# A two-layer decoder trunk on one core: where the stream's known part, the last keys and values, and the background products are queued

## The chip, the cores and the metric

One core of a Trainium2 chip runs the whole program. The metric is the device time of one execution in microseconds (us); the time given for a kernel is the median of several runs. The engines are called as in the profile: PE does matmuls (PEld is its loading of weights), DVE and ACT work elementwise, POOL does a few small things, and SP issues most of the loads from main memory.

## The reference

Batch 1, 256 tokens, width 2048, two layers, all in 32-bit floats. Layer 0 mixes by causal pooling, layer 1 by latent attention with 16 heads; both have a gated feed-forward part of inner width 5632. Each layer gets six modulation vectors from a conditioning vector `c`.

```python
sc = silu(c)
for i in range(2):
    shift_m, scale_m, gate_m, shift_f, scale_f, gate_f = split(sc @ mod_w[i] + mod_b[i], 6)
    if i == 1:
        kv_shift, kv_scale = split(sc @ kv_mod_w + kv_mod_b, 2)
        h_kv = modulate(rmsnorm(x, kv_in_norm), kv_shift, kv_scale)
        ckv = rmsnorm(h_kv @ w_dkv, kv_norm)
        k_nope, v, k_rope = ckv @ w_uk, ckv @ w_uv, rope(h_kv @ w_kr)
    h = modulate(rmsnorm(x, norm_mix[i]), shift_m, scale_m)
    if i == 0:
        y = pool_mixer(h, pool_w, pool_scale)
    else:
        cq = rmsnorm(h @ w_dq, q_norm)              # the query's latent
        q_nope, q_rope = split(cq @ w_uq); q_rope = rope(q_rope)
        p = softmax(causal((q_nope @ k_nope.T + q_rope @ k_rope.T) * SM_SCALE))
        y = (p @ v) @ w_o
    x = x + gate_m * y
    h = modulate(rmsnorm(x, norm_ffn[i]), shift_f, scale_f)
    x = x + gate_f * ((silu(h @ ffn_gate[i]) * (h @ ffn_up[i])) @ ffn_down[i])
return rmsnorm(x, final_norm)
```

## The kernel before

**Products in three parts.** A weight block of 512 x 512 is loaded by SP into one of six `raw` buffers and split: ACT writes an upper half (L440, a rounding to a matmul format), DVE the rest (L442, the difference). The activations are split likewise. A product is then the sum of upper x upper, upper x lower and lower x upper. One such block for both tiles of 128 tokens is 24 matmuls of 128 x 512 (`proj_unit`, L464): 16 need the upper half of the weight, and the last 8 the lower one. There are six buffers for halves, which is three blocks.

**The order of the work.** Outside of a few stretches that are ordered by hand, a scheduler in the compiler orders each engine's instructions ahead of time: it plays the program with modelled durations and lets each engine take, of those ready, the instruction that comes first in the program; some are marked as more urgent (the splits by 100 places). What it has ordered is a fixed queue on the chip. `tc.issue_after(ins)` says that what a block traces on the engine of `ins` is queued behind `ins`; it is an order in the queue and not a wait for the end of `ins`.

**Background.** The modulation vectors are computed on DVE beside the products: a unit loads 128 rows of a modulation weight and adds them, times one element of silu(c), to an accumulator (L230; L305 twice for a smaller block). A vector of 2048 has 16 units. When the last is done, `folded` sums the accumulator over partitions: four pieces on DVE (L320, L321) and then one small matmul (L326). The units stand in a list. Each split calls `tick`, which adds a rate to a credit and starts a unit for each whole credit; `plan(left, units)` sets the rate so that the list gets down to `left` within `units` splits, `hold` stops it, `release` goes on with a new rate. `behind` holds at most one instruction behind which units are queued. What must come later but is not urgent goes to `pending`; each split's `flush` runs what has come due, queued behind its two halves, and counts the rest down by one.

**The feed-forward part** runs over 11 chunks of 512 (`project_chunk`: gate, then up, four blocks each), turns them, and multiplies groups of them with the down weights (`down`), once per group and per 512 columns of the output. The sums of the groups go to `x`, whose old content is kept in memory beside (`aside`). At the start of the last chunk, `StreamEnd` loads the old stream back into `parts`. In the last group, `known` makes of each piece of 512 columns and 128 tokens what is known before the last products: `x * gate` (L673), added to the old stream (L674). `piece` then adds the last products. In the code, `known` stands at the last down-projection: for the first columns at its start, for the next ones behind the first split of each column block.

**Between the layers** (`then_attention`, ordered by hand) comes the key and value latent. Its norm and halves are made by the class `Latent`: the sum of squares on ACT (L1312), a power on POOL (L1314), a scaling on DVE (L1315), a turn on PE (L606), upper halves on ACT (L1325), lower halves on DVE (L1327). Then `keys_values(g)` makes the keys (`head_T`, L1363, 48 matmuls of 128 x 256) and values (24 of L464) of four heads at a time, g = 0 to 3. `hidden_q` turns and modulates one of four pieces of the hidden state for the queries; `modulated` first runs everything that is pending. The order in the code is: keys and values 0 and 1; keys 2; `last_of_background`, with the first `hidden_q`; values 2; the second `hidden_q`; the rotary key; the four blocks of `w_dq` (the query's latent) with the other two pieces; the latent's norm; keys 3; the latent's turn and halves (`query_latent`); values 3.

**The heads** go in eight pairs. For a pair, `project_heads` makes queries, with their rotary part through `rope_start` (ACT copies from PSUM, L912 and L914) and `rope_end` (DVE, L918, L919, L921); `probabilities` makes scores and softmax of each head (L1459 to L1477: exponentials on ACT, L1472 and L1473; a reciprocal on DVE, L1475; scaling on both); `turned` and `output` follow one pair later. The loop runs, for pair g: scores and softmax of g, turning of g-1, queries of g+2, output of g-1. The background is held while the first two pairs' queries are made, and then released.

After the heads come the output projection, whose sums are multiplied with the gate row `mla` (L736), and layer 1's feed-forward part.

## Time and profile before

| | us |
|---|---:|
| median of 3 runs (lowest, highest) | 1936.26 (1934.76, 1936.73) |
| the profiled execution's own time | 1935.94 |
| its span, first to last instruction | 1934.20 |
| PE busy | 1866.6 |
| DVE busy | 1482.1 |
| ACT busy | 849.2 |
| POOL busy | 49.4 |

The mean granted clock of PE is 0.983 over the span. Times in the profile count from the start of the span. In a line of groups stand the kernel's line, engine, operation, what is written and read, the shapes and the count; behind the bar the busy time in us and the mean duration of one in ns; then the engine's idle time just ahead of these instructions and what ended it. In a line of the timeline or of the chain stand the start, the time taken, and what ran. In a line of waits: who waited for whom, us in total, how often, the longest. A line by stretch has the stretch, its length and the busy time of each engine with the number of instructions; asked for one line of the kernel alone, it has only that line's. A pair of instructions in a row on DVE starts a little less apart than the duration of one.

### The profile page before, as it was taken

Reading aid. Unit: us, or ns where it says so; the run is one execution under the profiler, and the core shown is the slowest. Engines: PE = TensorE matmul, PEld = TensorE weight load, DVE = VectorE, ACT = ScalarE, POOL = GpSimd, SP = SyncE. Lnnn points to the kernel's source line nnn. Section 1 sums busy time; section 2 is a strip of 40 time slices with the busy share of each in tenths; the row PEclk is TensorE's granted clock in tenths of the full one; section 3 lists DMA queues with packets and bytes.
Section 4 is the critical chain, followed back from the end, with each engine's and each line's share of the span. In section 5 each row is a group of like instructions: output and inputs, shape, how many; then the busy total and the mean of one; then the engine's idle time right before and its main releaser. Section 6 shows DMA issues by size and latency. Waiting matters only on the chain.

```text
span 1934.2 us, 22338 instructions
## 1 busy us (share of the span) xinstructions
PE 1866.6 (97%) x8836; PEld 1511.7 (78%) x8836; DVE 1482.1 (77%) x1419; ACT 849.2 (44%) x954; POOL 49.4 (3%) x46
## 2 busy tenths in 40 slices
PE   6689999999999999999999999999999999999998
PEld 3156887888888888787879888888888888888887
DVE  2148899999878788888799986989886565555656
ACT  3024634443433344335678735634444433333333
POOL 0000000000000000001200000000000000000000
PEclk9689999999999999999999999999999999999999
DMA  9999999889898999998698695998886667666651
GB/s 397 411 416 387 386 364 320 303 308 362 322 344 318 339 336 331 353 337 273 214 341 297 213 332 187 386 334 312 279 291 239 231 240 255 235 205 236 218 196 44
DMA packets 226114, 575.08 MB, mean 297 GB/s; under 512 B 12109, under 2 KB 16709, under 8 KB 203859
## 3 DMA queue, kind: packets, MB, share of 16 engines
q1 hardware_dynamic: 225482, 570.49, 81.5%
q0 software_dynamic: 432, 3.15, 0.4%
q8 instruction: 69, 1.13, 0.2%
q14 instruction: 35, 0.29, 0.0%
q10 hardware_dynamic: 96, 0.02, 0.0%
HBM read 567.31 MB, written 6.32 MB: 297 GB/s over the span
## 4 chain that ended last, share of the span: by engine, by line
PE 89%; DMA 5%; DVE 3%; ACT 2%; issue 1%; POOL 0%; SPq 0%; POOLq 0%; DVEq 0%; ACTq 0%
PE ps L464 77%; DMA raw<-in_mod_w_dram 4%; PE ps L473 2%; PE ps L1048 2%; PE ps L1363 2%; PE ps L274 1%; PE ps L798 1%; DVE hl L442 1%; DMA act<-in_x_dram 1%; DVE acc L230 1%; PE ps L1271 1%; DMA raw<-in_ffn_up_dram 0%; PE ps L606 0%; PE ps L1023 0%; PE ps L840 0%
## 5 line engine op out<-in xcount | busy, mean ns | idle before, releaser
L464 PE MATMUL ps<-hl,act 128*128 128x512 f32 x6744 | 1549.7, 391 | 6.9 <-DVE hl L442 4.3
L464 PEld LDWEIGHTS ps<-hl,act 128*128 128x128 f32 x6744 | 1266.2, 188 | 271.5 <-DVE hl L442 5.2
L440 ACT ACTIVATE hl<-raw 128x2048 fp32r<-128x2048 f32 x289 | 552.9, 1917 | 619.9 <-PE ps L464 505.4
L442 DVE TENSOR_TENSOR hl<-raw,hl 128x2048 fp32r<-128x2048 f32 x289 | 660.7, 2288 | 201.4 <-ACT hl L440 200.6
L230 DVE SCALAR_TENSOR_TENSOR acc<-raw,s_col,acc 128x2048 f32<-128x2048 f32 x112 | 262.8, 2346 | 0.7 <-DMA raw<-in_mod_w_dram 0.6
L305 DVE SCALAR_TENSOR_TENSOR acc<-raw,s_col,acc 128x1024 f32<-128x1024 f32 x112 | 143.4, 1280 | 2.2 <-DMA raw<-in_mod_w_dram 0.7
L274 PE MATMUL ps<-raw,front 128*32 128x512 f32 x392 | 66.6, 744 | 25.6 <-DMA raw<-in_mod_w_dram 25.5
L767 DVE TENSOR_TENSOR act<-ps,act 128x512 f32<-128x512 f32 x96 | 64.1, 684 | 10.5 <-PE ps L464 10.2
L274 PEld LDWEIGHTS ps<-raw,front 128*32 128x32 f32 x392 | 9.7, 119 | 60.9 <-DMA raw<-in_mod_w_dram 48.4
L1363 PE MATMUL ps<-act,hl 128*128 128x256 f32 x384 | 48.8, 284 | 0.0
L473 PE MATMUL ps<-hl,act 128*128 128x512 f32 x192 | 47.0, 399 | 1.2 <-DVE act L569 0.9
L1363 PEld LDWEIGHTS ps<-act,hl 128*128 128x128 f32 x384 | 47.5, 192 | 0.7 <-DVE act L1327 0.2
L801 ACT ACTIVATE act<-ps 128x512 fp32r<-128x512 f32 x44 | 23.8, 595 | 52.6 <-PE ps L798 45.0
L281 DVE COPY t2k<-ps 128x256 f32<-128x256 f32 x4 | 1.7, 424 | 57.5 <-ACT t2k L280 57.5
L856 DVE TENSOR_TENSOR x<-ps,x 128x512 f32<-128x512 f32 x32 | 22.1, 691 | 30.1 <-PE ps L464 30.1
L473 PEld LDWEIGHTS ps<-hl,act 128*128 128x128 f32 x192 | 35.1, 188 | 10.9 <-ACT act L556 1.8
L867 ACT ACTIVATE t2k<-ps 128x512 f32<-128x512 f32 x24 | 14.2, 592 | 62.6 <-PE ps L464 62.5
L493 ACT ACTIVATE junk<-x 128x512 bf16<-128x512 f32 x23 | 14.6, 633 | 60.7 <-DVE x L681 39.9
L871 DVE TENSOR_TENSOR t2k<-ps,t2k 128x512 f32<-128x512 f32 x24 | 16.5, 688 | 25.3 <-PE ps L464 25.3
L1048 PEld LDWEIGHTS ps<-act,act 128*128 128x128 f32 x128 | 24.5, 198 | 11.5 <-issue 8.4
L1048 PE MATMUL ps<-act,act 128*128 128x256 f32 x128 | 31.7, 400 | 0.0
L802 DVE TENSOR_TENSOR act<-ps,act 128x512 fp32r<-128x512 f32 x44 | 28.2, 684 | 4.3 <-ACT act L801 4.1
(233 smaller groups left out, 1001.6 us busy)
## 6 DMA issues: line engine op xcount, KB each, us to landing
raw<-in_mod_w_dram SPq DMA_DIRECT2D x128, 1024.0 KB, 6.9
raw<-in_ffn_gate_dram SPq DMA_DIRECT2D x88, 1024.0 KB, 5.7
raw<-in_ffn_up_dram SPq DMA_DIRECT2D x88, 1024.0 KB, 6.5
raw<-in_ffn_down_dram SPq DMA_DIRECT2D x88, 1024.0 KB, 5.5
raw<-in_mod_w_dram SPq DMA_DIRECT2D x128, 512.0 KB, 6.5
raw<-in_kv_mod_w_dram SPq DMA_DIRECT2D x32, 1024.0 KB, 5.9
raw<-in_w_o_dram SPq DMA_DIRECT2D x16, 1024.0 KB, 8.8
raw<-in_w_uq_dram SPq DMA_DIRECT2D x8, 768.0 KB, 5.1
```

The lines of the kernel that those rows point to most:

```text
L230: dve.scalar_tensor_tensor(out=self.acc, in0=r, scalar=s_col[:, self.kt:self.kt + 1], in1=self.acc, op0=ALU.mult, op1=ALU.add)
L274: pe.matmul(self.bank[m * STRIP:(m + 1) * STRIP, :], lhsT=weights(k), rhs=r[:, k, i, :], start=first, stop=last)
L305: dve.scalar_tensor_tensor(out=self.acc, in0=r[:, k], scalar=s_col[:, self.kt + k:self.kt + k + 1], in1=self.acc, op0=ALU.mult, op1=ALU.add)
L440: hi_ins = act.activation(hi, r, AF.Copy)
L442: lo_ins = dve.tensor_tensor(out=lo, in0=r, in1=hi.bitcast(F32), op=ALU.subtract)
L464: pe.matmul(banks[tok], lhsT=t_[:, i, k, tok * P:(tok + 1) * P], rhs=w[:, k, :], start=first and n < len(part), stop=last and n >= len(ord ...
L473: pe.matmul(bank, lhsT=t_[:, i, k, tok * P:(tok + 1) * P], rhs=w[:, k, :], start=first and n == 0, stop=last and n == len(order) - 1)
L767: dve.tensor_tensor(out=part, in0=banks[tok], in1=part, op=ALU.add)
L801: act.activation(m[:, 0, :, ts_], v, AF.Copy)
L802: dve.tensor_tensor(out=m[:, 1, :, ts_], in0=v, in1=m[:, 0, :, ts_].bitcast(F32), op=ALU.subtract)
L1048: pe.matmul(mixed[g][:, n % 2, :], lhsT=wp[g][:, k, ns], rhs=pool_all[g // 2][:, g % 2, k, :], start=k == 0, stop=k == KL - 1)
L1363: pe.matmul(pt[:, h, :], lhsT=w(h0 + h, k), rhs=t_[:, i, k, :], start=n == 0, stop=n == 3 * KL - 1)
```

## The change

It has five parts. The first: `known` takes one piece (128 tokens, 512 columns), and its eight calls in a layer go to `pending` at the start of the last chunk, one due at each of the chunk's eight splits. The second: `last_of_background` comes after values 2 instead of between keys 2 and values 2, and keys 3 come before the query latent's sums, with the second `hidden_q` and the new `plan` behind the keys. The third: values 3 are made for the first 128 tokens, then `query_latent` (turn and halves) comes, then those of the second 128 tokens. The fourth: after each softmax, `behind` is set to its last instruction on DVE, so that the units started by later splits are queued behind it; it is cleared ahead of the output projection. The fifth: in `rope_start` DVE multiplies the sums in PSUM by the cosine directly, instead of ACT copying them and DVE multiplying the copy in `rope_end`.

```diff
@@ class StreamEnd
-            self.known(0)
-
-        def known(self, j):
+        def known(self, j, tok, gate):
 
             js = slice(j * CH, (j + 1) * CH)
-            for tok in range(NT):
-                part, piece = self.parts[tok][:, js], x[:, tok, js]
-                dve.tensor_tensor(out=piece, in0=piece, in1=self.gate[:, js], op=ALU.mult)
-                dve.tensor_tensor(out=part, in0=piece, in1=part, op=ALU.add)
+            part, piece = self.parts[tok][:, js], x[:, tok, js]
+            dve.tensor_tensor(out=piece, in0=piece, in1=gate[:, js], op=ALU.mult)
+            dve.tensor_tensor(out=part, in0=piece, in1=part, op=ALU.add)
@@ down
-                    if last and c == g[0]:
-                        end.known(j + 1)
@@ project_chunk
             if c == NF - 1:
-                stream_end.append(StreamEnd(l))
+                end = StreamEnd(l)
+                stream_end.append(end)
+                for n, (j, tok) in enumerate((j, tok) for j in range(ND) for tok in range(NT)):
+                    pending.append((n, lambda j=j, tok=tok: end.known(j, tok, gates[gate_name])))
@@ rope_start
-        act.activation(t_[:, 0, :], bank, AF.Copy)
+        dve.tensor_tensor(out=t_[:, 0, :], in0=bank, in1=cos_t, op=ALU.mult)
@@ rope_end
-        dve.tensor_tensor(out=t_[:, 0, :], in0=t_[:, 0, :], in1=cos_t, op=ALU.mult)
@@ keys_values
-    def keys_values(g, between=None):
+    def keys_values(g, between=None, within=None):
...
-        vb = proj(a["w_uv"][:, gs], [ckvT])
+        if within is None:
+            vb = proj(a["w_uv"][:, gs], [ckvT])
+        else:
+            vb = [ps_t() for _ in range(NT)]
+            hi, lo = w_unit(a["w_uv"][:, gs])
+            for tok in range(NT):
+                proj_unit(vb, ckvT, hi, lo, True, True, (tok,))
+                if tok == 0:
+                    within()
@@ attention
     for g in range(1, H // KG - 1):
-        kv.append(keys_values(g, last_of_background if g == H // KG - 2 else None))
-    hidden_q()
+        kv.append(keys_values(g))
+    last_of_background()
...
-    plan(n_all - n_mix - WO_LATE, HEAD_UNITS)
-    cq = [ps_t() for _ in range(NT)]
-    for j in range(ND):
-        if len(hmx) < ND:
-            hidden_q()
-        hi, lo = w_unit(a["w_dq"][0][j * CH:(j + 1) * CH, :])
-        proj_unit(cq, hmx[j], hi, lo, j == 0, j == ND - 1)
-    end, cqT = Latent(cq, V_QN), []
-    for tok in range(NT):
-        end.norm(tok)
+    cq, cqT = [], []
+    end = None
+
+    def query_sums():
+        nonlocal end
+        plan(n_all - n_mix - WO_LATE, HEAD_UNITS)
+        cq.extend(ps_t() for _ in range(NT))
+        hidden_q()
+        for j in range(ND):
+            if len(hmx) < ND:
+                hidden_q()
+            hi, lo = w_unit(a["w_dq"][0][j * CH:(j + 1) * CH, :])
+            proj_unit(cq, hmx[j], hi, lo, j == 0, j == ND - 1)
+        end = Latent(cq, V_QN)
+        for tok in range(NT):
+            end.norm(tok)
...
-    kv.append(keys_values(H // KG - 1, query_latent))
+    kv.append(keys_values(H // KG - 1, query_sums, query_latent))
@@ probabilities
-        dve.tensor_scalar(out=s_[:, 1:3, :], in0=s_[:, 1:3, :], scalar1=rl[:, 1:2], scalar2=None, op0=ALU.mult)
+        behind[:] = [dve.tensor_scalar(out=s_[:, 1:3, :], in0=s_[:, 1:3, :], scalar1=rl[:, 1:2], scalar2=None,
+                                       op0=ALU.mult).ins]
@@ after the heads
+    behind.clear()
     plan(n_late, WO_UNITS)
```

## The prediction

> **What bounds the kernel now.** I read the page first, then the waits, then the busy time by stage.

> ```profile
> span 1934.2 us, 22338 instructions
> ...
> PE 1866.6 (97%) x8836; PEld 1511.7 (78%) x8836; DVE 1482.1 (77%) x1419; ACT 849.2 (44%) x954; POOL 49.4 (3%) x46
> ...
> DVE  2148899999878788888799986989886565555656
> ...
> L464 PE MATMUL ps<-hl,act 128*128 128x512 f32 x6744 | 1549.7, 391 | 6.9 <-DVE hl L442 4.3
> ...
> L230 DVE SCALAR_TENSOR_TENSOR acc<-raw,s_col,acc 128x2048 f32<-128x2048 f32 x112 | 262.8, 2346 | 0.7 <-DMA raw<-in_mod_w_dram 0.6
> ```

> PE is the bound. The change removes no matmul, so it can only win the moments in which PE stands still or runs slowly. Past the front of the kernel these are few. PE's own waits, asked for in three stretches (800 to 830 us, 970 to 990 us, 1030 to 1095 us), give

> ```profile
> PE ps L464 <- DVE hl L442: 4.3, 1, 4.3
> ...
> PE ps L326 <- issue: 4.3, 1, 4.3
> ...
> PE ps L1483 <- ACT t2k L1476: 3.1, 2, 1.6
> ```

> The first lies where the last chunk of layer 0 begins, the second among the shared keys and values, the third (two waits) among the heads. The busy time around them (stretch, its length, busy us of PE, PEld, DVE, ACT, POOL, then the granted clock, DMA share, GB/s):

> ```profile
> 814.40:905.00 90.60, 86.30 (x377) 70.60 (x376) 83.75 (x68) 36.87 (x34) 1.81 (x1) 0.96 0.94 334
> ...
> 818.10:822.40 4.30, 0.03 (x1) 0.00 (x0) 4.27 (x6) 1.91 (x1) 0.00 (x0) 0.87 1.03 408
> 822.40:829.00 6.60, 6.57 (x17) 5.22 (x18) 6.53 (x5) 1.91 (x1) 0.00 (x0) 0.57 1.02 367
> ...
> 976.90:981.10 4.20, 0.00 (x0) 0.00 (x0) 4.20 (x9) 3.05 (x3) 0.00 (x0) 1.00 1.01 392
> 981.10:985.00 3.90, 3.86 (x11) 3.16 (x12) 3.83 (x6) 1.09 (x3) 0.95 (x1) 0.57 0.84 272
> ...
> 1043.90:1054.50 10.60, 9.10 (x67) 8.53 (x66) 10.16 (x24) 9.98 (x28) 0.00 (x0) 1.00 0.70 243
> 1054.50:1063.40 8.90, 8.90 (x67) 8.53 (x66) 8.07 (x19) 8.31 (x23) 0.00 (x0) 1.00 0.61 224
> ```

> Two things are to be seen. DVE is nearly full in all these stretches, so an edit that takes PE's waits away squeezes the same DVE work into less time. And after each of the two long gaps the granted clock is 0.57, while it stays at 1.00 after the 1.5 us gap among the heads: a long gap is paid twice.

> **Edit 1: the stream's known part.** The chain of waits, and when the sixteen instructions of L673 (multiplies) and L674 (additions) ran in layer 0 (DVE busy, count):

> ```profile
> 820.09 2.29 DVE hl L442
> ...
> 822.43 3.78 PE ps L464 x8
> ...
> 764.00:812.00 48.00, 4.13 (x6) 1.00 0.88 327
> ...
> 812.00:820.10 8.10, 5.08 (x8) 1.00 1.04 408
> ```

> Though the code places `known` in the last down-projection, the compiled order has pulled six multiplies up into the down-projection before it, and all eight additions into one heap from 812 to 820 us. The lower half of the last chunk's first weight (L442 at 820.09) stands behind that heap, and PE behind L442. After the change each pair of instructions is queued behind one of the eight splits of that chunk, so the first L442 goes ahead of all of them. The 4.30 us go, and the slow clock with them: from 822.4, 17 matmuls took 6.6 us, and at full speed (24 in 5.47 us, the row of 964.79 below) need 3.9, so 2.7 more. To win: 7.0 us.

> What is late next is DVE, busy 83.8 of 90.6 us from 814.4 to 905. Six multiplies and two additions that ran ahead of this stretch come into it, 8 x 0.69 (4.13 us for 6) = 5.5 us, and its length shrinks by 7.0: 89.3 us of work for 83.6, less 1 us that L442 gains by its earlier start. A background product (L230) that slips past the stretch costs nothing; one that has to be done before the next layer's hand-over costs its time. So 0 to 4.7 us come back. I take 2.5, the middle, as no row says which. **Edit 1: -4.5 us, between -7.0 and -2.3.** In layer 1 the last slices of the DVE row show 5 to 6 tenths busy, and the same pieces cost nothing there.

> **Edit 2: last keys ahead of the query's latent.** The chain and DVE's work at the second gap:

> ```profile
> 964.79 5.47 PE ps L464 x24
> ...
> 981.14 0.41 PE ps L326 x2
> 981.55 7.14 PE ps L464 x24
> ...
> 974.02 2.28 DVE L442 TENSOR_TENSOR hl<-raw,hl 128x2048 fp32r<-128x2048 f32 x1
> ...
> 979.81 1.23 DVE L321 TENSOR_REDUCE acc<-t2k 128x16 f32<-128x512 f32 x2
> ```

> L326 closes the fold of a modulation vector. It stands in PE's queue ahead of the third group's values (the 24 matmuls of 981.55), whose weights were split by 976.3, and waits for the fold's last piece, done at 981.0. With `last_of_background` behind the values, these run first: 976.9 + 5.5 for them + 0.9 for the turn = 983.3 us, 2 us after the fold. Won: 4.2 us of gap and 7.14 - 5.47 = 1.7 us of slow clock, 5.9. Behind the turn now stand the last keys; their lower half takes the place of the first query weight's, right after the fold, so PE may wait some 0.3 us. On SP's queue the last keys' load passes the four query weights, which it delays by one load; these have the keys' 5.8 us more of time. **Edit 2: -5.6 us, between -5.9 and -4.**

> **Edit 3: last values around the latent.** It takes cover away:

> ```profile
> 1013.76 5.75 PE ps L1363 x48
> 1019.51 0.87 PE ps L606 x8
> ...
> 1024.02 1.18 DVE act L1327 x3
> ...
> 1017.74 0.75 DVE L1315 TENSOR_SCALAR t2k<-ps,sm 128x512 f32<-128x512 f32 x1 [0.44 <-POOL sm L1314]
> ...
> 940.57 0.60 ACT L1312 ACTIVATE junk<-ps 128x512 bf16<-128x512 f32 x1 [0.28 <-PE ps L1271]
> ...
> 942.71 0.75 DVE L1315 TENSOR_SCALAR t2k<-ps,sm 128x512 f32<-128x512 f32 x1 [0.73 <-POOL sm L1314]
> ```

> Now the norm runs from 1013.8 to 1018.5, 4.7 us under 5.75 us of keys; the halves from the turn's end, 1020.4, to 1025.2, 4.8 us under 24 matmuls of values. Afterwards each has 12 matmuls, 2.7 us, for cover. With chains as long as now PE waits 2.0 + 2.1 = 4.1 us. Both are stretched by DVE, though: the key's latent went through the same norm in 3.0 us (940.5 to 943.5), which leaves a wait of 0.3, and two L230 leave this stretch (edit 4). Of 0.3 to 4.1 us I take **+1.5**, nearer to the key's row.

> **Edit 4: background behind softmaxes.** The first gap among the heads by the timeline, the weight split ahead of the second, and the background products run before the softmaxes:

> ```profile
> 1042.65 2.34 DVE L230 SCALAR_TENSOR_TENSOR acc<-raw,s_col,acc 128x2048 f32<-128x2048 f32 x1
> ...
> 1043.10 0.19 ACT L1473 ACTIVATION_READ_ACCUMULATOR t2k<-t2k,sm 128x1 f32 x1
> ...
> 1044.91 0.16 DVE L1475 RECIPROCAL sm<-sm 128x2 f32<-128x2 f32 x1
> ...
> 1045.88 0.33 PE L1483 MATMUL ps<-con,t2k 128*128 128x128 f32 x1 [1.50 <-ACT t2k L1476]
> ...
> 1079.79 2.28 DVE L442 TENSOR_TENSOR hl<-raw,hl 128x2048 fp32r<-128x2048 f32 x1
> ...
> 1025.00:1036.00 11.00, 5.91 (x3) 1.00 0.94 308
> ```

> The reciprocal could go at 1043.3 and stood 1.6 us behind L230. Queued behind the softmax, L230 can't do that: -1.5. The other gap has a weight split (L442) in front of its reciprocal and stays. The price is crowding. The plan now starts one split later, so five units instead of seven run before the heads, and the three from 1025 to 1036 us may not run ahead any more. Of 19 units 14 are left, 1.75 to a pair of heads, in whole units 1, 2, 2, 2, 1, 2. A pair lasts 8.90 us on PE and holds, beside one L230 of 2.35, 5.7 us of DVE work. Six pairs need 6 x 5.7 + 10 x 2.35 = 57.7 us for 53.4 us of PE: 4.3 us too much, less at most the 5.9 us by which DVE is freer at their start. I take +1.0. **Edit 4: -0.5, between -1.5 and +4.** The last gate unit, and so the gate row, ends up to a pair later; its consumer comes after the heads. No row prices that: 0 here, up to 3 us in the range.

> **Edit 5: rotary cosine from PSUM.** DVE's nine products stay nine, ACT loses nine copies that no PE wait names:

> ```profile
> L802 DVE TENSOR_TENSOR act<-ps,act 128x512 fp32r<-128x512 f32 x44 | 28.2, 684 | 4.3 <-ACT act L801 4.1
> L673 DVE TENSOR_TENSOR x<-x,gate 128x512 f32<-128x512 f32 x16 | 11.0, 689 | 0.3
> ```

> A product with one side in PSUM (L802) takes no longer than one in SBUF (L673): 0. [...]

> **The sum** against the profiled execution's 1935.94 us (span 1934.20 and 1.74 around it): -4.5 - 5.6 + 1.5 - 0.5 = -9.1, so 1926.8. The median of the runs, 1936.26, lies 0.3 above that execution: **1927.1 us**.

> **Rivals.** *A: DVE binds the last chunk.* All 4.7 us come back: 1929.3. If the fold there, delayed by the new pieces, also holds PE as L326 does at 977, 4.2 more: 1933.5. For it: 83.8 of 90.6 us. Against it: L230 and the fold yield to L442 in the compiled order.

> *B: edit 3's two waits become one.* If the compiled order puts the second half of the values ahead of the turn, the 4.1 us stand in one piece and the clock falls after it (1.7 to 2.7 us): 6.5 instead of 1.5, 1932.1. [...]

> *C: slower, the heads become DVE's.* Behind the softmax no background fills DVE while ACT does the exponentials:

> ```profile
> L1473 ACT ACTIVATE t2k<-t2k,sm 128x256 f32<-128x256 f32 x16 | 7.9, 494 | 0.0
> L1472 ACT ACTIVATE t2k<-t2k,sm 128x128 f32<-128x128 f32 x16 | 6.4, 397 | 4.6 <-DVE sm L1469 4.3
> ```

> With the accumulator reads (0.19 each, row of 1043.10) that is 1.27 us a head, 2.5 a pair. Wholly unfilled, a pair with two units takes 5.7 + 4.7 + 2.5 = 12.9 us, one with a single unit 10.6: 4 x 4.0 + 2 x 1.7 = 19.4 us more, the total 1936.3 - 4.5 - 5.6 + 1.5 - 1.5 + 19.4 = 1945.6. Half filled, 10.3 less: about 1937. It decides for slower by 0.2% once the pairs average over 11.2 us. Against it: weight splits and rotary products are free to fill.

> *D: all gaps close, nothing comes back*: -7.0 - 5.9 - 1.5, and -1.6 for the second gap among the heads, = -16.0: 1920.3.

> **How the numbers follow.** A measurement here tells 0.2%, 3.9 us, from no change (the runs span 2.0 us). Forecast 0.53, A 0.13, B 0.12, C 0.14, D 0.08. Faster means under 1932.4: forecast, D, half of A, half of B, minus the forecast's own upper tail, 0.72. Slower means over 1940.1: most of C, 0.10. Between: 0.18. The range, 1920 to 1936, starts at D and leaves out C's upper part.

> **What would show it.** In the changed kernel: no PE wait on L442 near 818 us and the clock at 1.00 there; the known products in pairs behind L442; no PE wait at L326 among the keys; two PE waits under 2.1 us each at the last values; L1475 not behind L230, and pairs of about 9 us. I am wrong if PE stands over 3 us at any of these places or pairs last over 10 us.

## The result and the profile after

The changed kernel takes **1952.0 us** (median of 4 runs, 1950.81 to 1954.34), the kernel before 1936.5 beside it: a ratio of 1.0083, 95% interval 1.0065 to 1.0100. It is slower by 0.8%, where 1927.1 was forecast. The profiled execution took 1954.34 us, the longest of the four. The page after, with the lines that answer to those of before:

```profile
span 1952.5 us, 22317 instructions
...
PE 1873.6 (96%) x8836; PEld 1515.4 (78%) x8836; DVE 1482.0 (76%) x1419; ACT 846.4 (43%) x945; POOL 47.1 (2%) x46
...
L464 PE MATMUL ps<-hl,act 128*128 128x512 f32 x6744 | 1549.9, 391 | 12.2 <-DVE act L1517 6.4
```

The span is 18.3 us longer, and PE is busy only 7.0 us more: the rest is standing still. PE's waits in the three stretches that the prediction named, widened to hold what took their place (800 to 870, 970 to 990, 1030 to 1140 us; engine, line, what it waited for, sum, times, longest):

```profile
PE ps L795 <- DVE t2k L869: 2.7, 1, 2.7
PE ps L464 <- DVE hl L442: 1.9, 2, 1.4
...
PE ps L326 <- DVE acc L321: 3.3, 1, 3.3
...
PE ps L1496 <- ACT t2k L1488: 6.9, 5, 2.8
PE ps L464 <- DVE act L1517: 6.4, 1, 6.4
```

(After the change L1471 stands for L1459, L1476 for L1464, L1485 for L1473, L1487 for L1475, L1488 for L1476, L1496 for L1483, L1517 for L1504.) No stretch is free of waits. The 4.3 us at the last chunk have become 4.6 in three pieces, the 4.3 at the fold 3.3, and among the heads and behind them stand 13.3 where 3.4 stood. The busy time in four stretches, the second of them a part of the third, before and then after (stretch, length, busy us of PE, PEld, DVE, ACT, POOL, granted clock, DMA share, GB/s):

```profile
835.00:870.00 35.00, 35.00 (x164) 29.03 (x163) 29.80 (x25) 12.61 (x12) 1.81 (x1) 1.00 0.92 332
1000.00:1040.00 40.00, 40.00 (x255) 36.48 (x254) 38.78 (x45) 28.78 (x54) 3.45 (x2) 1.00 0.94 331
1000.00:1112.00 112.00, 108.67 (x715) 99.33 (x714) 107.31 (x189) 89.47 (x213) 3.45 (x2) 1.00 0.76 265
1112.00:1136.00 24.00, 24.00 (x110) 19.86 (x109) 18.26 (x19) 8.49 (x10) 1.57 (x2) 1.00 0.99 355
```

```profile
835.00:870.00 35.00, 31.53 (x137) 25.38 (x138) 34.90 (x35) 14.43 (x12) 1.81 (x1) 0.95 0.90 327
1000.00:1040.00 40.00, 39.60 (x230) 34.68 (x229) 30.57 (x45) 30.59 (x57) 1.10 (x2) 1.00 0.65 221
1000.00:1112.00 112.00, 104.69 (x655) 94.71 (x654) 92.72 (x169) 83.23 (x196) 1.10 (x2) 0.97 0.64 222
1112.00:1136.00 24.00, 17.58 (x85) 14.10 (x85) 23.18 (x29) 9.72 (x20) 0.95 (x1) 0.91 0.68 231
```

Read them against each other. From 835 to 870 DVE went from 29.8 to 34.9 of 35 us: it is the bound there, and PE lost 3.5 us. From 1000 to 1112, in the last values and the heads, DVE did 14.6 us *less*: it stood idle 19.3 us instead of 4.7. More than half of that, 8.2 us, lies ahead of 1040 us, where the first exponentials run: the background products (L230) fill 4.7 us there instead of 16.4. What DVE waited for the exponentials from 1000 to 1112 us is a smaller part, 0.9 us before and this after:

```profile
DVE sm L1487 <- ACT t2k L1485: 4.5, 5, 1.5
```

Most of the other idle time ends with other results of ACT, as the upper halves of weights (5.3 us) and the rotary copies (2.6). From 1112 to 1136 DVE is full and PE stands. So the same engine is short of time in one place and idle in the next. The pace of the pairs says where the time goes, by the first score of the fifth to the eighth pair after the change:

```profile
1068.97 0.39 PE L1471 MATMUL ps<-act,act 128*128 128x128 f32 x2
...
1083.85 0.39 PE L1471 MATMUL ps<-act,act 128*128 128x128 f32 x2
...
1097.38 0.39 PE L1471 MATMUL ps<-act,act 128*128 128x128 f32 x2
...
1102.71 0.39 PE L1471 MATMUL ps<-act,act 128*128 128x128 f32 x2
```

Up to the fifth pair the changed kernel is on time (before, that pair's first score stood at 1069.69), so DVE's idle time up to there has not yet cost PE anything. Then a pair takes 14.9 and 13.5 us instead of 8.9 and 10.7, and the tail behind the heads takes the rest. In the first of these two PE waits 1.2 and 2.9 us for the turns of the fourth pair. Two held products (1061.94 and 1064.81) stand on DVE ahead of that pair's masks (L1478, 1067.40), where the kernel before has them at 1063.48.

### The profile page after: what moved, and what is told of

It is laid out like the page before. It is cut to its first block, busy times and chain, and to the rows that moved or that the text cites. A ratio compares the mean times of both kernels' runs of the same rounds, so it can differ in the third digit from the quotient of the medians.

```text
span 1952.5 us, 22317 instructions
## 1 busy us (share of the span) xinstructions
PE 1873.6 (96%) x8836; PEld 1515.4 (78%) x8836; DVE 1482.0 (76%) x1419; ACT 846.4 (43%) x945; POOL 47.1 (2%) x46
## 4 chain that ended last, share of the span: by engine, by line
PE 85%; DVE 6%; DMA 5%; ACT 1%; issue 1%; POOL 0%; SPq 0%; DVEq 0%; POOLq 0%; ACTq 0%
PE ps L464 73%; DMA raw<-in_mod_w_dram 4%; DVE hl L442 2%; PE ps L274 2%; PE ps L1369 2%; PE ps L473 2%; PE ps L1046 2%; DVE acc L230 1%; PE ps L795 1%; DVE acc L305 1%; PE ps L1269 1%; DMA raw<-in_w_o_dram 1%; DMA raw<-in_ffn_up_dram 0%; DMA t2k<-in_mod_b_dram 0%; DVE acc L321 0%
## 5 line engine op out<-in xcount | busy, mean ns | idle before, releaser
L464 PE MATMUL ps<-hl,act 128*128 128x512 f32 x6744 | 1549.9, 391 | 12.2 <-DVE act L1517 6.4
L464 PEld LDWEIGHTS ps<-hl,act 128*128 128x128 f32 x6744 | 1264.1, 188 | 278.7 <-DVE act L1517 6.8
L442 DVE TENSOR_TENSOR hl<-raw,hl 128x2048 fp32r<-128x2048 f32 x289 | 660.5, 2287 | 196.8 <-ACT hl L440 196.2
L230 DVE SCALAR_TENSOR_TENSOR acc<-raw,s_col,acc 128x2048 f32<-128x2048 f32 x112 | 262.6, 2344 | 0.8 <-DMA raw<-in_mod_w_dram 0.7
L764 DVE TENSOR_TENSOR act<-ps,act 128x512 f32<-128x512 f32 x96 | 64.0, 683 | 10.5 <-PE ps L464 10.2
L1369 PE MATMUL ps<-act,hl 128*128 128x256 f32 x384 | 52.8, 298 | 0.0
L1369 PEld LDWEIGHTS ps<-act,hl 128*128 128x128 f32 x384 | 51.5, 207 | 0.7 <-DVE act L1325 0.2
L473 PEld LDWEIGHTS ps<-hl,act 128*128 128x128 f32 x192 | 35.1, 188 | 10.7 <-ACT act L556 1.8
L493 ACT ACTIVATE junk<-x 128x512 bf16<-128x512 f32 x23 | 14.5, 632 | 63.0 <-DVE x L678 40.2
L869 DVE TENSOR_TENSOR t2k<-ps,t2k 128x512 f32<-128x512 f32 x24 | 16.5, 687 | 23.9 <-PE ps L464 23.8
L762 ACT ACTIVATE act<-ps 128x512 f32<-128x512 f32 x32 | 19.1, 596 | 28.4 <-PE ps L464 28.1
```

What stands on the lines that cost most here:

```text
L230: dve.scalar_tensor_tensor(out=self.acc, in0=r, scalar=s_col[:, self.kt:self.kt + 1], in1=self.acc, op0=ALU.mult, op1=ALU.add)
L442: lo_ins = dve.tensor_tensor(out=lo, in0=r, in1=hi.bitcast(F32), op=ALU.subtract)
L464: pe.matmul(banks[tok], lhsT=t_[:, i, k, tok * P:(tok + 1) * P], rhs=w[:, k, :], start=first and n < len(part), stop=last and n >= len(ord ...
L473: pe.matmul(bank, lhsT=t_[:, i, k, tok * P:(tok + 1) * P], rhs=w[:, k, :], start=first and n == 0, stop=last and n == len(order) - 1)
L764: dve.tensor_tensor(out=part, in0=banks[tok], in1=part, op=ALU.add)
L1369: pe.matmul(pt[:, h, :], lhsT=w(h0 + h, k), rhs=t_[:, i, k, :], start=n == 0, stop=n == 3 * KL - 1)
```

## The experiments

The kernel before ran beside each set of experiments, with medians between 1934.9 and 1935.3 us; ratios are to it, with 95% intervals. "Free" kernels are the changed kernel without edit 4.

**The parts alone.** First edit 4 undone, then edit 4 alone (e2 makes the same edit on the kernel before):

```diff
-        behind[:] = [dve.tensor_scalar(out=s_[:, 1:3, :], ... op0=ALU.mult).ins]
+        dve.tensor_scalar(out=s_[:, 1:3, :], ... op0=ALU.mult)
```

*e1, edit 4 undone.*

> The changed kernel with edit 4 undone: background products are free to run ahead of a softmax again. Theory (edit 4 costs nearly all: held products keep their raw tiles, the load queue waits behind them, weights come late): the 14 us lost between the first scores and the last head output and the 4 behind it go, about 1937. Rival 1 (edits 1 to 3 lose it, edit 4 only shows it): above 1946. The forecast of this document for edits 1 to 3 and 5: about 1927.6.

Measured 1934.76 us, ratio 0.9998 (0.9989 to 1.0007). The difference from the changed kernel is edit 4's: 17.2 us between the medians, 16.5 by the two ratios, as the kernel before stood at 1936.5 us beside the changed kernel and at 1935.3 here. The other four edits together gain nothing that can be told from zero.

*e2, edit 4 alone.*

> The kernel before with edit 4 alone. Theory (edit 4 costs by itself): about 1952 to 1954, with the load queue waiting for L230 among the heads. Rival (edit 4 costs only together with the plan that starts one split later, edits 2 and 3): about 1938 to 1942.

Measured 1947.23, 1.0060 (1.0045 to 1.0075): 12 us by itself, 5 more in the company of the others. Both forecasts were missed, each by about 5 us: the measured time lies between them.

*e3, edit 1 alone* (its three hunks on the kernel before).

> The kernel before with edit 1 alone: the stream's known part in pairs behind the splits of the last chunk. Theory (DVE binds the last chunk, the gain of the 4.3 us gap comes back before the hand-over): 1935 to 1938. The forecast of this document: 1932. If the clock's recovery is won and kept: 1929.5.

Measured 1935.27, 0.9997 (0.9988 to 1.0007): nothing. In its trace PE stands 1.41, 0.53 and 2.75 us at 834, 848 and 863 us, as after the full change.

**What in the hold costs.** e4 holds the background behind the softmax's maximum, so that DVE may take a product while ACT does the exponentials:

```diff
-        dve.tensor_tensor(out=nmx[:, 1:2], in0=nmx[:, 1:2], in1=nmx[:, 2:3], op=ALU.min)
+        behind[:] = [dve.tensor_tensor(out=nmx[:, 1:2], ... op=ALU.min).ins]
```

> The changed kernel with the background held behind the maximum of the softmax, not behind its last product: DVE may take a background product while ACT does the exponentials. If edit 4 costs because DVE stands idle under the exponentials: about 1938. If it costs because a held product keeps a raw tile and so the queue of loads: the hold is 2 us shorter of 9, and 1946 to 1950 remain.

Measured 1944.46, 1.0047 (1.0030 to 1.0064): 7.5 us come back, 9.7 remain, below the range of the second theory and above the number of the first. From 1000 to 1112 us the two kernels without the hold, or with a shorter one, read (e1, then e4):

```profile
1000.00:1112.00 112.00, 109.39 (x700) 98.57 (x700) 107.54 (x191) 89.01 (x213) 1.86 (x3) 1.00 0.73 250
```

```profile
1000.00:1112.00 112.00, 106.94 (x679) 96.06 (x678) 97.48 (x182) 83.20 (x205) 1.09 (x2) 1.00 0.70 234
```

DVE's idle time there is 4.5 us in e1, 14.5 in e4, 19.3 after, and the totals are 0, 9.7 and 17.2 us above e1's. The order is the same, but that does not make the idle time the price: e9 below does not fit it.

The changed trace offers another cause: loads. ACT waits for weights (1030 to 1140 us), which it never did there before:

```profile
ACT hl L1450 <- DMA raw<-in_w_uq_dram: 6.5, 2, 3.9
ACT hl L440 <- DMA raw<-in_w_o_dram: 4.3, 3, 2.5
```

A held product keeps its raw tile, and the loads in SP's queue wait for one: from 1030 to 1140 us that queue waited 20.7 us for L230 after the change, 5.2 before. e5 and e6 are a pair that differ in edit 4 alone, with one raw tile more and one split tile less:

```diff
-        return work.tile(shape, dt, tag="raw", bufs=6, name=nm("raw"))
+        return work.tile(shape, dt, tag="raw", bufs=7, name=nm("raw"))
...
-        return work.tile(shape, dt, tag="hl", bufs=6, name=nm("hl"))
+        return work.tile(shape, dt, tag="hl", bufs=5, name=nm("hl"))
```

*e5, with edit 4:*

> The changed kernel, edit 4 included, with seven raw tiles instead of six and five split tiles instead of six. To be compared with the next run, which differs from it in edit 4 alone. Theory (a held product keeps a raw tile, the queue of loads waits for it): with one tile more edit 4 costs half or less of the 17.2 us that it costs with six, 4 to 9 us. Rival (DVE, idle under the exponentials and crowded behind them, is what costs): edit 4 costs as much as with six, 14 to 18.

*e6, without:*

> The same seven raw and five split tiles without edit 4: the base of the run before this one. No theory has a number for the five split tiles; with six of each this kernel took 1934.8. A ring of five may cost up to 10 us.

Measured 1956.34, 1.0112 (1.0096 to 1.0127), and 1940.20, 1.0028 (1.0019 to 1.0038). Edit 4 costs 16.1 us here too, although ACT's waits for weights among the heads have shrunk to one of 1.7 us (e5, L1450).

So the raw tiles alone don't make the price: with most of the late loads gone it stays. The pair is not a clean test, as e6 takes 5.4 us more than e1, and in the changed trace one late load does hold a pair: ACT's split L1450 waited 3.9 us for it, up to 1069.66, and the fourth pair's exponentials stood behind that split.

*e9 and e10*: three units ahead of the heads in the program's order, with and without edit 4, so that no softmax holds them:

```diff
+    pump(3)
     hold()
     heads = [project_heads(g) for g in range(2)]
```

> The changed kernel, edit 4 included, with three background units taken ahead of the heads in the program's order, so that no softmax holds them. Theory (the hold empties VectorE before the first softmax, 8.4 us idle from 1000 to 1035 against 1.2 to 2.3 without it, and the three products that ran there crowd the heads and end behind them): 3 x 2.35 = 7 us come back, about 1945. Rival (the idle time of VectorE under the exponentials alone costs): 1950 to 1952.

> The same three units ahead, without edit 4: the base of the run before. Theory: these products ran ahead of the first softmax anyway, so 1934 to 1936, as without the three units ahead.

Measured 1951.21, 1.0084 (1.0070 to 1.0098), and 1935.85, 1.0004 (0.9995 to 1.0013). The products did run earlier, and it was worth 0.8 us between the medians and nothing by the ratios (1.0084 and 1.0083), not 7: this theory falls as well. It also shows that DVE's idle time is no measure of the price. In e9 it is 11.9 us, less than in e4, and the kernel takes 6.8 us more than e4:

```profile
1000.00:1112.00 112.00, 97.23 (x624) 88.16 (x623) 100.14 (x176) 80.13 (x196) 3.40 (x2) 0.94 0.71 242
```

But its trace shows a wait of PE in one piece (7.5 us at L1503), and so does e2's, here by the timeline (start, us, engine, line):

```profile
1091.77 4.73 DVE L230 SCALAR_TENSOR_TENSOR acc<-raw,s_col,acc 128x2048 f32<-128x2048 f32 x2
...
1096.46 2.29 DVE L442 TENSOR_TENSOR hl<-raw,hl 128x2048 fp32r<-128x2048 f32 x1
1098.67 1.30 DVE L320 STREAM_TRANSPOSE t2k<-acc 128x512 f32<-128x512 f32 x2
1099.89 1.24 DVE L321 TENSOR_REDUCE acc<-t2k 128x16 f32<-128x512 f32 x2
1100.57 1.08 ACT L1486 ACTIVATE t2k<-ps 128x384 f32<-128x384 f32 x2 [1.85 <-DVE acc L321]
...
1101.11 1.22 PE L1491 MATMUL ps<-t2k,act 128*128 128x256 f32 x2 [8.07 <-ACT t2k L1486]
```

A background vector ends here. Its last two products have waited for the softmax, its fold (L320, L321) stands behind them on DVE, and the fold keeps t2k tiles. The copy of the turned probabilities (L1486) needs such a tile, so it waits for L321, and PE 8.07 us for the copy. e13, e14 and e15 give the fold one raw tile instead, on the changed kernel, on the free one and on e2:

```diff
+        big = None if pieced[0] else raw_t([P, n])
...
-            tr, ns = t2k([P, CH]), slice(i * CH, (i + 1) * CH)
+            tr = t2k([P, CH]) if big is None else big[:, ns]
```

> The changed kernel, edit 4 included, with the fold's turned pieces in one raw tile instead of four t2k tiles, wherever the fold is not spread over splits. Theory (the hold pushes the end of a background part and its fold behind a softmax; the fold keeps t2k tiles that the turned copies need, and PE waits for these): half of the 17 us go, 1940 to 1946. Rival (the idle time of VectorE under the exponentials and the crowding behind it cost all): 1950 to 1953.

> The same tiles without edit 4, the base of the run before. Without the hold no copy waits for a fold among the heads, so 1934 to 1937.

> The kernel before with edit 4 alone and the fold in a raw tile. With t2k tiles it took 1947.2 and PE waited 8.1 us for a turned copy that waited for the fold's pieces. Theory (t2k tiles kept by the fold): that wait goes, 1938 to 1941. Rival: 1946 to 1948.

Measured 1952.67, 1.0091 (1.0077 to 1.0105); 1942.51, 1.0039 (1.0025 to 1.0052); 1941.29, 1.0032 (1.0021 to 1.0044). On e2 the 8 us wait is gone and 5.9 us with it. On the free kernel the other tile costs 7.7 us by itself, which I had not expected, and e13 stands at the rival's number; against its own base e14, edit 4 costs 10.2 us there instead of 17.2. So the fold's tiles are a part of the cost in e2; how large a part in the changed kernel, these three do not settle, as the remedy has a price of its own.

**Edit 1.** If DVE binds the last chunk, taking the known products off it must help. e7 puts them on GpSimd in the free kernel:

```diff
-            dve.tensor_tensor(out=piece, in0=piece, in1=gate[:, js], op=ALU.mult)
-            dve.tensor_tensor(out=part, in0=piece, in1=part, op=ALU.add)
+            pool.tensor_tensor(out=piece, in0=piece, in1=gate[:, js], op=ALU.mult)
+            pool.tensor_tensor(out=part, in0=piece, in1=part, op=ALU.add)
```

> The changed kernel without edit 4, and the sixteen known products of each layer on GpSimd, which is idle there, instead of VectorE. Theory (VectorE binds the last chunk of layer 0 with edit 1: 34.9 of 35 us busy from 835 to 870): 11 us of its work go, the waits at 834, 848 and 863 us (4.7 together) go with them, about 1930, unless GpSimd takes more than 2.5 us for a product and the pieces come late. Rival (the waits come from elsewhere, as from loads): 1934 to 1936.

Measured 1932.20, 0.9986 (0.9977 to 0.9995): 2.6 us less than e1, though the two intervals still overlap. In place of the three waits one of 2.13 us stands in e7, for L442 at 837 us.

**Edits 2, 3 and 5.** The fold still held PE at 982 us. The timeline of DVE after the change shows why:

```profile
978.96 0.70 DVE L320 STREAM_TRANSPOSE t2k<-acc 128x512 f32<-128x512 f32 x1
979.58 2.25 DVE L442 TENSOR_TENSOR hl<-raw,hl 128x2048 fp32r<-128x2048 f32 x1
981.75 0.68 DVE L321 TENSOR_REDUCE acc<-t2k 128x16 f32<-128x512 f32 x1
982.34 0.70 DVE L320 STREAM_TRANSPOSE t2k<-acc 128x512 f32<-128x512 f32 x1
982.97 2.25 DVE L442 TENSOR_TENSOR hl<-raw,hl 128x2048 fp32r<-128x2048 f32 x1
985.14 0.68 DVE L321 TENSOR_REDUCE acc<-t2k 128x16 f32<-128x512 f32 x1
...
985.87 0.69 PE L326 MATMUL ps<-acc,con 128*128 128x64 f32 x2 [3.31 <-DVE acc L321]
```

The last keys stand close behind now, so their weight splits (L442) are due early and the compiled order puts two of them in between the fold's pieces. Two attempts on the free kernel: e8 moves the fold's end behind the last keys, e11 gives its pieces priority over splits.

```diff
     for g in range(1, H // KG - 1):
         kv.append(keys_values(g))
-    last_of_background()
...
         nonlocal end
+        last_of_background()
         plan(n_all - n_mix - WO_LATE, HEAD_UNITS)
```

> The changed kernel without edit 4, with the last background call moved from behind the third values to the start of the query's sums, behind the last keys. Theory (the product that closes the fold waits because two weight splits went ahead of the fold's last pieces; behind 5.8 us of keys it finds them done): the 2.65 us wait goes, 1931 to 1932.5. Rival (the wait moves again, to the turn of the hidden state for the query's first sums, which needs the fold's columns): 1934 to 1936.

Measured 1942.49, 1.0039 (1.0024 to 1.0054), slower than either forecast: PE waits 1.37 us at L326 all the same, then 3.91 and 2.16 us at turns (L606).

```diff
             if pieced[0]:
                 pending.append((i // 2 if n_ == 2 else i, lambda i=i: piece(i)))
+            elif hurry[0]:
+                with tc.high_priority(offset=200):
+                    piece(i)
             else:
                 piece(i)
```

> The changed kernel without edit 4, with the pieces of the fold among the shared keys at a priority above the weight splits. Theory (two weight splits that went in between the fold's pieces keep the closing product waiting, 2.65 us): the wait goes and up to 1 us comes back at the last keys' lower half, 1932.5 to 1933.5. Rival (the splits that are now later hold PE instead): 1934 to 1936.

> The changed kernel without edit 4, with the known products on GpSimd and the fold's pieces first: the two gains together if they are in series, as waits at 862 and 981 us on PE are: 1932.2 less 1.3 to 2.3, 1930 to 1931.

(`hurry` is set from the first shared keys to the last background call; e12 has e7's edit too.) Measured 1934.46, 0.9994 (0.9985 to 1.0003), and 1932.22, 0.9982 (0.9973 to 0.9990). The wait at L326 is gone in both, and nothing is won over e1 and e7: PE waits 1.24 us at the last keys and 2.60 us at the first pair's turns instead, in e11.

*e16, edits 2 and 3 alone:*

> The kernel before with edits 2 and 3 alone. The forecast of this document: 1932.2 (-5.6 and +1.5). Theory (the wait for the fold moves from the values to the last keys, since two weight splits go in between the fold's pieces): 1.0 to 1.5 us less, 1934.

Measured 1931.88, 0.9984 (0.9975 to 0.9993). So they do gain 3.0 us, where 4.1 was forecast; and in e1 that gain is lost to edit 1 or edit 5. e17 and e18 leave edit 5 out (its three lines as before), e18 with the known products on GpSimd:

> The kernel before with edits 1, 2 and 3: the changed kernel without edits 4 and 5. Theory (edit 5 turned the compiled order of VectorE at the fold among the keys, a weight split went ahead of the fold's last piece, and the gain of edits 2 and 3 was lost by that): without edit 5 the fold ends ahead of the split, as with edits 2 and 3 alone, and the time is 1931 to 1932.5. Rival (edit 1 takes the gain): 1934 to 1936.

> The same with the known products on GpSimd. If what that gained beside edit 5 (2.6 us) adds: 1929 to 1930. If only what it gained up to the hand-over (898.6 against 900.0 us): 1930.5.

Measured 1932.25, 0.9986 (0.9977 to 0.9994), and **1930.65, 0.9977 (0.9968 to 0.9987)**. Edit 1 leaves the gain alone; edit 5 takes 2.5 us (e1 against e17), and 1.6 us with the known products on GpSimd (e7 against e18). The intervals of each two overlap a little, and no run has edit 5 alone, so its size is uncertain. DVE around the fold in e17:

```profile
980.99 0.70 DVE L320 STREAM_TRANSPOSE t2k<-acc 128x512 f32<-128x512 f32 x1
981.72 0.42 DVE L920 TENSOR_TENSOR krT<-t2k 64x256 f32<-64x256 f32 x1
982.17 0.69 DVE L321 TENSOR_REDUCE acc<-t2k 128x16 f32<-128x512 f32 x1
982.78 2.28 DVE L442 TENSOR_TENSOR hl<-raw,hl 128x2048 fp32r<-128x2048 f32 x1
...
982.91 0.43 PE L326 MATMUL ps<-acc,con 128*128 128x64 f32 x2 [0.47 <-DVE acc L321]
```

One 0.42 us step of the rotary key (L920) still stands there, the second split goes behind the fold, and the wait is 0.47 instead of 3.31 us. That this order is where edit 5's 2.5 us lie is what the traces suggest, not shown: e11 mended that wait with edit 5 in place and gained nothing. e18 beats both kernels, the one before by 0.23%.

## Why the prediction was wrong, step by step

**Edit 4 (-0.5; rival C): the step that failed**, with +17.2 us in this kernel and +12 alone. The term that was mis-sized is the price, the crowding, taken as +1.0: 4.3 us too much work for DVE in six pairs, less up to 5.9 us by which DVE would be freer at their start. That free time came and passed unused, since a held product can't run in it: DVE stood idle 9.4 us from 1000 to 1040, 1.2 before and 2.7 without the hold (e1). The loss came later, 6.0 and 2.8 us longer for the fifth and the sixth pair, where held products stand in front of the next softmax, and then behind the heads. Rival C had a part of the mechanism, DVE idle under the exponentials, and wholly unfilled it gave 1945.6. It was held unlikely (0.14) because "weight splits and rotary products are free to fill". They filled only in part, as DVE's wait for the exponentials rose from 0.9 to 4.5 us; but that is far from the 17.2, so the rival was not right either. e4 shows how much the last part of the hold, from the softmax's maximum to its end, is worth: 7.5 us. And both the forecast and the rival counted only the time that DVE lacks in a pair; neither saw that a held product also holds what stands behind it on DVE, the fold with its t2k tiles (e2: 8.07 us of PE in one wait), nor the backlog that DVE is left with behind the heads. That backlog is the 6.4 us at L1517 after the change: ACT had its upper half ready at 1127.2, and in DVE's timeline the lower half stands behind three background products and two splits:

```profile
1127.05 1.27 DVE L305 SCALAR_TENSOR_TENSOR acc<-raw,s_col,acc 128x1024 f32<-128x1024 f32 x1
1128.24 2.28 DVE L442 TENSOR_TENSOR hl<-raw,hl 128x2048 fp32r<-128x2048 f32 x1
1130.44 1.27 DVE L305 SCALAR_TENSOR_TENSOR acc<-raw,s_col,acc 128x1024 f32<-128x1024 f32 x1
1131.64 2.28 DVE L442 TENSOR_TENSOR hl<-raw,hl 128x2048 fp32r<-128x2048 f32 x1
1133.84 1.27 DVE L305 SCALAR_TENSOR_TENSOR acc<-raw,s_col,acc 128x1024 f32<-128x1024 f32 x1
1135.04 0.68 DVE L1517 TENSOR_TENSOR act<-ps,act 128x512 fp32r<-128x512 f32 x1
```

What edit 4 could win at the reciprocal is bounded by the 3.1 us that PE waits at L1483 in the kernel before, and without the hold 1.6 us of it are left (e1). How the 17.2 us divide between idle DVE, tiles kept by the fold, late loads and the backlog stays open.

**Edit 1 (-4.5; rival A 1929.3): the rival's mechanism was right, its size too small.** The 4.30 us went, with the slow clock (0.84 from 814 to 835 us before, 1.00 after), and all of it came back as waits for a full DVE: 0.0 alone (e3), +0.4 beside edits 2 and 3 (e17 against e16). The upper bound of the sum, 4.7 us back, was still too small. DVE has time earlier and later, but not between 835 and 870. e7 and e18, with this work off DVE, are 2.6 and 1.6 us faster than e1 and e17, which agrees.

**Edits 2 and 3 (-5.6 and +1.5): about right in sum, by themselves.** They gave -3.0 (e16) for -4.1; no run has one without the other, so neither term is tested alone. The step from "these run first" to "2 us after the fold" took DVE's order for fixed; it moves with its surroundings, which is why the fold holds PE 0.5 us in e16 and 3.3 in the changed kernel. Rival B's long wait did not come: at the last values the longest is 0.4 us in the changed kernel and 1.0 in e1.

**Edit 5 (0): off by some 2.5 us**, not by the price of the instruction. After the change the product from PSUM (L911) took 416 ns and its neighbour from SBUF (L917) 420:

```profile
L917 DVE TENSOR_TENSOR t2k<-t2k,sin_t 128x256 f32<-128x256 f32 x9 | 3.8, 420 | 2.6 <-ACT t2k L913 2.6
L911 DVE TENSOR_TENSOR t2k<-ps,cos_t 128x256 f32<-128x256 f32 x9 | 3.7, 416 | 0.4 <-PE ps L1458 0.4
```

The compiled order differs with it (e1 and e17 at the fold), and "0" left no range for that.

The sum as measured: -3.0 (2 and 3), +0.4 (1), +2.5 (5), +17.2 (4) = +17.1. Each term leads from one run to the next, so their sum is no check of the terms. The changed kernel stood 15.5 us above the kernel before that ran beside it.

## What to carry to other kernels

Before holding filler work behind a critical chain, ask what fills the engine while that chain runs on another one, and what stands behind the filler in the same queue: its tiles and its followers are held with it, and what was held comes out in a row, here in front of the next softmax (1061.94 and 1064.81 us). An edit that frees one engine's wait is worth only the slack, in that stretch, of the engine that feeds it: here the 4.30 us wait went, and e3 gained nothing, with DVE busy 34.9 of 35 us after the full change. And where a compiler orders the queues, cost no edit at zero (edit 5 here: 2.5 us, e1 against e17): time each part alone as well as together.

## What the hardware showed unexpectedly

```profile
837.36:839.40 2.04, 2.04 (x5) 1.67 (x6) 2.04 (x1) 0.00 (x0) 0.00 (x0) 0.50 1.02 395
```

```profile
835.20:837.20 2.00, 1.98 (x9) 1.64 (x10) 2.00 (x1) 0.60 (x1) 0.00 (x0) 1.00 1.08 399
...
865.75:869.00 3.25, 3.25 (x10) 2.77 (x11) 3.25 (x4) 2.10 (x2) 0.00 (x0) 0.51 0.80 297
```

```profile
865.80:869.00 3.20, 3.20 (x16) 2.75 (x17) 3.20 (x4) 2.41 (x2) 0.00 (x0) 1.00 0.74 289
```

  Elsewhere in the changed kernel it was 0.50 in the 2 us after PE's waits of 3.31 us (985.90 to 988.00) and 6.39 us (1135.80 to 1138.00); after 2.85 us it was 0.68 from 1076.40 to 1078.40 and 0.50 in the next 2 us. So to count two waits of 2.0 and 2.1 us at no loss of clock was not safe.
- **GpSimd took 2.8 to 3.3 times as long for the known part's two steps** (1.93 and 2.25 us in e7) as DVE (0.69 us each), and beside it DVE was slower: from 814 to 905 us L442 took 2454 ns on average in e7 and 2285 in e1, which differs from e7 in this edit alone. The move seems to pay all the same: e7 and e18 are the faster ones beside e1 and e17, with intervals that overlap (e7, then e7's DVE in that stretch, then e1's):

```profile
L671 POOL TENSOR_TENSOR act<-x,act 128x512 f32<-128x512 f32 x16 | 35.8, 2254 | 12.3 <-DMA act<-aside 11.8
L670 POOL TENSOR_TENSOR x<-x,gate 128x512 f32<-128x512 f32 x16 | 30.8, 1926 | 107.9 <-DVE x L851 107.7
```

```profile
L442 DVE TENSOR_TENSOR hl<-raw,hl 128x2048 fp32r<-128x2048 f32 x16 | 39.2, 2454 | 1.5 <-ACT hl L440 1.5
```

```profile
L442 DVE TENSOR_TENSOR hl<-raw,hl 128x2048 fp32r<-128x2048 f32 x16 | 36.6, 2285 | 0.0
```
